# A one-core encoder trunk: down projection regrouped into parts of 6, 4, 8 and 4 tiles, and a new price list for the planner

## The chip, the cores and the metric

The kernel runs on one core of a Trainium2 chip. The metric is device time in microseconds (us). Three runs of the kernel before gave 1074.99, 1075.91 and 1076.12 us, median 1075.91. Engines are named as the profile names them: PE (matrix products) with PEld (its weight loads), DVE, ACT, POOL and SP; SP and POOL also issue the transfers (DMA).

## What is computed

A layer works on 512 prompt tokens and 64 sample tokens, 576 columns of 1024 features:

```
x += Mixer(RMSNorm(x))       # gated delta rule (4 heads) and gated linear attention (4 heads), gated merge
x += CrossAttn(RMSNorm(x))   # 4 heads into 256 memory tokens
x += ConvFFN(RMSNorm(x))     # what the change touches
y  = RMSNorm(x)

def conv_ffn(h):                               # D_FF = 2816 = 22 tiles of 128
    u = h @ w_up                               # (576, 2*2816): gate half and value half
    u = causal_dwconv(u, width=3) + conv_b
    return (silu(u_gate) * u_val) @ w_down     # (576, 2816) @ (2816, 1024)
```

Recurrent states, the last rows of both convolutions and the memory keys and values are outputs too.

## The kernel before

**Arithmetic.** Everything is held feature-major: a tile is 128 features by the 576 token columns. Weights and activations are float32, and each is split into a high and a low half (`w` tiles hold both; `xh`/`xl`, `ach`/`acl` and `hl` are activations), so that one product of 128 features costs three matmuls: high by high, low by high, high by low. A **plain** product handles the 576 columns as two matmuls of 256 and 320 columns (2 x 290 in the up projection, which pads to 580). **Seven products** handle a pair of output tiles at once: columns are halved (288, or 290), input tiles are taken in pairs, and the eight block products of a 2 x 2 by 2 x 2 block multiplication are replaced by seven (named P1, Q5, P2, Q6, P3, Q7, Q4). It needs sums of weight blocks (`ws` tiles, four sums for a pair, made on DVE), sums of activations (`tu`, `tw`, made in `operands`), and seven additions of results instead of four.

**Feed-forward stage.** `up j` makes gate tile j and value tile 22 + j from `yops` (products) or from `yx` (plain); the result goes through the norm's scale (`fu<-fu,rbc`), three taps of the convolution (`fc`), SiLU and the gate product, and is split again (`acl<-fc,ach`). `down (m, p)` multiplies part p of those 22 tiles into output tile m of x. `PARTS` (L96) cuts the 22 tiles into four parts, here of 6, 6, 4 and 6. `NPLAIN` (L128) is the count of plain up pairs, `DNPLAIN` (L129) names the parts whose down products are plain, and `DNAT` (L130) says after which up pair how many pairs of the part before are multiplied. Of the last part, tiles 2 to 5 go as seven products, tiles 0, 1 ("last") and 6, 7 (`half`, L2318) plain. `ffn_order` (L135) turns this into one fixed list.

**Weights.** A weight comes by a DMA into a `wr` tile; ACT writes the high half (CAST) and minus the weight (ACTIVATE) and POOL issues a DMA that adds the weight again (`split_summed`, L717), or ACT writes the high half of a sum and DVE (at times POOL) subtracts (`w<-ws,w`). There are ten `w` tiles and four `wr` tiles (L30 to L33), and 64 slots (`NS`, L29) for all other wide tiles.

**What sets the order.** A planner in the program (`Driver`) keeps a clock for every engine while the kernel is written down. PE's instructions stand in the order in which `main` yields them, with the steps of side chains (the delta rule `c_gdn`, the norms, the attention) slipped in when the planner has their inputs ready. An instruction of DVE, ACT or POOL is booked into the first gap of its engine after its inputs are ready (`place`, L374); with a rank from `URGENT` (L40) it may push lower ones back (`ahead`, L405). The engine then gets its instructions in the order of the planned starts. `weigh` (L219) prices an instruction; `HOP` (L35) is the delay assumed from one engine's end to another's start; `note` (L447) and `hold` (L482) book. The planner's prices thus set the order of instructions and nothing else: every wait on the chip is a semaphore on the real producer.

Of the kernel before, what the change touches and what calls it, by code (L numbers as in the profile page):

```python
# [31 lines left out]
WF = 4  # L32
RF = 1  # L33
NGDN = 2
HOP = 0.2  # L35
BACK = 6.0
MARGIN = 0.6
LAG = 0.0
# [54 lines left out]

PARTS = [list(range(0, 6)), list(range(6, 12)), list(range(12, 16)), list(range(16, 22))]  # L96
PARTK = [p[0::2] + p[1::2] for p in PARTS]
PART0 = [0, 6, 12, 16]
def product_order(pairs, whole=False):


# [23 lines left out]
XAT = ("qb", 1)  # L125
XLAG = 30.0
GPAIRS = [(("gta", m), ("gtb", m)) for m in range(GPLAIN, 8)]
NPLAIN = 3  # L128
DNPLAIN = (0, 1, 2)  # L129
DNAT = (0,) * 6, (0, 0, 0, 2, 1, 1), (0, 2, 1, 1), (0, 0, 0, 0, 1, 1)  # L130
UPAIRS = [(("up", j), ("up", NJ + j)) for j in range(NPLAIN, NJ)]
HALVED = {t for p in GPAIRS + WPAIRS + MPAIRS + UPAIRS for t in p}

# [76 lines left out]
class Engine:  # L210
# [8 lines left out]
    def weigh(self, calls):  # L219
        cost, aps, outs = 0.0, [], []  # L220
        for name, args, kw in calls:
            a = [v for v in list(args) + list(kw.values()) if hasattr(v, "tensor")]
            ins = [v for v in a[1:] if free(v) > 1]
            n = max(free(v) for v in a)
            if kw.get("op") == ALU.pow:
                cost += 0.3 + 0.165 * free(a[0])
            else:
                twice = self.key == "V" and len(ins) == 1 and self.port([(name, args, kw)])
                cost += self.drv.FIXED[self.key] + n * self.drv.PACE[self.key] * (0.5 if twice else 1.0)
            cost += 0.06 * (name == "scalar_tensor_tensor" or self.key == "V" and a[0].shape[-1] <= 128 and any(v.space == bass.MemoryType.PSUM for v in a[1:]))  # L230
            cost += 0.2 * (kw.get("accum_out") is not None) + 0.09 * hasattr(kw.get("scale"), "tensor")
            outs.append(a[0])
            if kw.get("accum_out") is not None:
                outs.append(kw["accum_out"])
            aps += a
        return cost, outs, aps
# [11 lines left out]

    def when(self, calls):
        cost, outs, aps = self.weigh(calls)  # L250
        return self.drv.place(self.key, self.drv.open(outs, aps), cost, False, self.port(calls)) + cost

    def together(self, calls, extra=0.0):

        cost, outs, aps = self.weigh(calls)
        self.drv.note(self.key, cost + extra, outs, aps, [(getattr(self.eng, name), args, kw) for name, args, kw in calls], self.port(calls))


class Either:
# [20 lines left out]
class Driver:  # L280

    FIXED = dict(V=0.15, A=0.17, G=0.2, D=0.01)
    PACE = dict(V=1 / 960, A=1 / 1180, G=1 / 465, D=512 / 320e3)

# [117 lines left out]
    def ahead(self, key, t, cost, port=False, op=None):  # L405

        q = self.busy[key]
        t = max(t, self.now - BACK)
        i = 0
        while i < len(q):  # L410
            o = q[i]
# [5 lines left out]
            if o.start < t or o.level >= op.level:  # L417
                t, i = o.end, i + 1
# [9 lines left out]
            if stuck is None:  # L428
                for o, at in moves:
                    self.shift(o, at)  # L430
                break
            t, i = q[i].end, i + 1
        self.book_op(q, op, t, cost, port)
        q.sort(key=lambda o: o.start)
        return t
# [11 lines left out]
    def note(self, key, cost, outs, aps, fns, port=False):  # L447
        op = Op()
        t = self.open(outs, aps)
        op.level = self.urgent  # L450
        start = (self.ahead if op.level else self.place)(key, t, cost, port=port, op=op)
        end = start + cost
        self.before(start, outs, aps)
        self.mark(self.wrote, end, outs, op)
        self.mark(self.seen, end, aps, op)
# [26 lines left out]
    def hold(self, fn, cost, args, kw):  # L482
# [4 lines left out]
        self.put(self.now, [(fn, args, kw)])  # L487
        self.now += cost
        self.mark(self.seen, self.now, ins)
        self.mark(self.wrote, self.now, [out])  # L490
        self.last = max(self.last, self.now)
        self.flush(self.now - BACK)

    def array(self, out, lhsT, rhs, exact=True):
# [6 lines left out]
        self.mode, self.half = mode, None if beside else at  # L501
        if beside:
            return 0.01
        return turn + (max(n * 0.0004375 + 0.008, 0.109) if fast else 0.107 if not exact else max(n * 4 / 2400, 0.107))

    def matmul(self, out, lhsT, rhs, **kw):
        self.hold(self.pe.matmul, self.array(out, lhsT, rhs), (out, lhsT, rhs), kw)
# [2085 lines left out]
```

## Time and profile before

| | |
|---|---|
| median of three runs | 1075.91 us |
| profiled execution, its own time | 1073.67 us |
| span of that execution, first to last instruction | 1071.9 us |
| mean granted clock of PE, as a share of 2.4 GHz | 0.997 |
| PE busy | 1059.0 us, 99% |
| DVE busy | 779.2 us, 73% |
| ACT busy | 722.9 us, 67% |
| POOL busy | 336.0 us, 31% |

Almost every operation is recorded by one helper line (L314), so groups are told apart by their tiles: `bank` and `sm` are PSUM tiles, `w` weights, `x` the residual stream, `fu` and `fc` the up projection before and inside its convolution. Matmul records overlap (each shows its whole pipeline), so the pace of PE is read from the distance of starts and not from the mean of one. The feed-forward stage runs from about 667 us to the end.

### The profile page before, as it was taken

To read this page: it belongs to the slowest core of one execution; us is meant where nothing else is said; L and a number is where in the kernel's file an instruction comes from. 1 tells how busy PE (TensorE), PEld (TensorE's weight loads), DVE (VectorE), ACT (ScalarE), POOL (GpSimd) and SP (SyncE) were. 2 spreads that over 40 slices of the span, in tenths; PEclk is the share of its full clock that TensorE was granted. 3 is DMA by queue.
4 is the path that set the end of the run, shared out by engine and by line. 5 is a ranking of instruction groups with operands and counts; after the bars stand their busy time and mean duration, and the time that the engine had idled before them with its cause. 6 is when DMAs were issued, how large, how long until landed. Compare 5 with 4: busy or idle time off the path is not lost.

```text
span 1071.9 us, 21256 instructions
## 1 busy us (share of the span) xinstructions
PE 1059.0 (99%) x8086; PEld 1041.1 (97%) x8086; DVE 779.2 (73%) x1518; ACT 722.9 (67%) x1435; POOL 336.0 (31%) x529
## 2 busy tenths in 40 slices
PE   9999999999999999999999999999999999999997
PEld 8999999999999999999999999999999999999996
DVE  5776657677786869877647777888885765788874
ACT  7767456765766766465755768877876666687753
POOL 2343045322433224121110134334434233333420
PEclk9999999999999999999999999999999999999999
DMA  8854137643366987688873558758898798878863
GB/s 279 188 119 102 29 99 179 174 101 82 63 150 140 205 231 199 209 190 221 220 196 91 127 141 199 173 120 183 172 214 191 156 191 185 176 159 169 195 125 104
DMA packets 67813, 172.77 MB, mean 161 GB/s; under 512 B 7872, under 2 KB 14912, under 8 KB 67712
## 3 DMA queue, kind: packets, MB, share of 16 engines
q0 software_dynamic: 30816, 71.32, 39.1%
q1 hardware_dynamic: 36752, 100.09, 28.7%
q8 instruction: 64, 1.05, 0.4%
q14 instruction: 37, 0.30, 0.1%
q10 hardware_dynamic: 144, 0.00, 0.0%
HBM read 158.81 MB, written 5.37 MB: 153 GB/s over the span
## 4 chain that ended last, share of the span: by engine, by line
PE 93%; DMA 2%; DVE 2%; issue 1%; ACT 1%; POOL 1%; SPq 0%; DVEq 0%; POOLq 0%; ACTq 0%
PE bank L314 62%; PE sm L314 31%; DMA wr<-wt 1%; DMA w<-wt 1%; DMA vec<-vec 1%; DVE ws L314 0%; ACT w L314 0%; ACT sq L314 0%; POOL rr L314 0%; DVE w L314 0%; SPq L314 0%; DVE c L314 0%; DVE gt L314 0%; DVE rr L314 0%; ACT xh L314 0%
## 5 line engine op out<-in xcount | busy, mean ns | idle before, releaser
L314 PE MATMUL bank<-xh,w 128*128 128x320 f32 (+3 forms) x1664 | 316.9, 300 | 2.5 <-DVE u L314 1.7
L314 PE MATMUL bank<-ach,w 128*128 128x256 f32 (+3 forms) x1362 | 268.9, 296 | 0.0
L314 PEld LDWEIGHTS bank<-xh,w 128*128 128x128 f32 x1664 | 254.9, 189 | 4.4 <-ACT e L314 1.9
L314 POOL DMA_DIRECT2D w<-wt x152 | 133.9, 890 | 372.2 <-ACT w L314 296.0
L314 PEld LDWEIGHTS bank<-ach,w 128*128 128x128 f32 x1362 | 216.1, 188 | 0.7 <-issue 0.3
L314 PE MATMUL bank<-xl,w 128*128 128x256 f32 (+2 forms) x832 | 188.4, 296 | 0.3 <-DVE xl L314 0.3
L314 ACT CAST w<-wr 128x512 fp32r<-128x512 f32 (+4 forms) x208 | 157.9, 762 | 26.1 <-PE bank L314 19.7
L314 PE MATMUL bank<-acl,w 128*128 128x288 f32 (+3 forms) x681 | 168.1, 295 | 0.0
L314 ACT ACTIVATE w<-wr 128x512 fp32r<-128x512 f32 (+3 forms) x186 | 141.7, 763 | 9.8 <-PE bank L314 7.5
L314 PEld LDWEIGHTS bank<-xl,w 128*128 128x128 f32 x832 | 142.4, 189 | 0.6 <-DVE xl L314 0.6
L314 PE MATMUL sm<-ach,w 128*128 128x290 f32 (+1 forms) x618 | 133.2, 296 | 0.6 <-DVE x L314 0.6
L314 PEld LDWEIGHTS bank<-acl,w 128*128 128x128 f32 x681 | 121.8, 188 | 0.0
L314 ACT CAST w<-ws 128x512 fp32r<-128x512 f32 (+1 forms) x144 | 87.0, 610 | 28.7 <-DVE ws L314 13.4
L314 PEld LDWEIGHTS sm<-ach,w 128*128 128x128 f32 x618 | 102.6, 189 | 1.2 <-ACT w L314 0.8
L314 DVE TENSOR_TENSOR w<-ws,w 128x512 fp32r<-128x512 f32 (+1 forms) x112 | 75.7, 682 | 12.8 <-ACT w L314 12.0
L314 PE MATMUL sm<-acl,w 128*128 128x290 f32 (+1 forms) x309 | 84.7, 296 | 0.0
L314 DVE SCALAR_TENSOR_TENSOR fc<-fu,vec,fc 128x578 f32<-128x578 f32 x88 | 70.9, 816 | 4.5 <-ACT fc L314 4.0
L314 PEld LDWEIGHTS sm<-acl,w 128*128 128x128 f32 x309 | 58.2, 188 | 0.0
L314 DVE TENSOR_TENSOR x<-x,bank 128x256 f32<-128x256 f32 (+2 forms) x73 | 30.0, 442 | 28.2 <-PE bank L314 28.0
L314 DVE TENSOR_TENSOR ws<-ws,wr 128x512 f32<-128x512 f32 (+1 forms) x72 | 48.8, 678 | 0.4
L314 POOL DMA_DIRECT2D w<-wd x34 | 29.6, 872 | 61.6 <-ACT w L314 60.7
L314 ACT ACTIVATE fc<-fu,vec 128x578 f32<-128x578 f32 x44 | 38.3, 873 | 15.0 <-POOL fu L314 14.9
(394 smaller groups left out, 2066.2 us busy)
## 6 DMA issues: line engine op xcount, KB each, us to landing
wr<-wt SPq DMA_DIRECT2D x134, 512.0 KB, 5.4
w<-wt POOLq DMA_DIRECT2D x102, 256.0 KB, 5.5
w<-wt POOLq DMA_DIRECT2D x50, 512.0 KB, 7.0
wr<-wd SPq DMA_DIRECT2D x24, 384.0 KB, 5.3
w<-wd POOLq DMA_DIRECT2D x20, 384.0 KB, 6.4
w<-ws POOLq DMA_DIRECT2D x26, 256.0 KB, 3.8
x<-xT SPq DMA_DIRECT2D x16, 288.0 KB, 6.4
y<-xT SPq DMA_DIRECT2D x8, 288.0 KB, 5.7
```

The costliest lines, as they stand in the source:

```text
L314: fn(*args, **kw)
```

## The change

It does two things. First, the 22 tiles are cut into parts of 6, 4, 8 and 4 instead of 6, 6, 4 and 6; the second part (4 tiles) is multiplied as seven products for all four pairs of output tiles; the last part stays half and half; and one up pair more goes as seven products (two plain pairs instead of three). `DNAT` is set anew. Second, the planner's prices change: `HOP` falls from 0.2 to 0.06 with 0.14 (`PELAT`) added behind a matmul; each DVE and ACT instruction occupies its engine for 0.085 and 0.095 less than its result takes (`TAIL`); a scan costs twice per column; a DVE instruction with two SBUF inputs that is booked by rank starts after a POOL instruction that is under way (`VEXT`), and a POOL instruction grows by the DVE instructions that it overlaps (`GEXT`); a one-column matmul in full float32 costs 0.218.

```diff
-HOP = 0.2
+HOP = 0.06
+PELAT = 0.14
+GEXT = 1.0
+VEXT = True
...
-PARTS = [list(range(0, 6)), list(range(6, 12)), list(range(12, 16)), list(range(16, 22))]
+PARTS = [list(range(0, 6)), list(range(6, 10)), list(range(10, 18)), list(range(18, 22))]
-PART0 = [0, 6, 12, 16]
+PART0 = [0, 6, 10, 18]
...
-NPLAIN = 3
-DNPLAIN = (0, 1, 2)
-DNAT = (0,) * 6, (0, 0, 0, 2, 1, 1), (0, 2, 1, 1), (0, 0, 0, 0, 1, 1)
+NPLAIN = 2
+DNPLAIN = (0, 2)
+DNAT = (0,) * 6, (0, 0, 2, 2), (0, 0, 2, 2, 0, 0, 0, 0), (0, 0, 1, 1)
...
+            cost += n * self.drv.PACE[self.key] * (name == "tensor_tensor_scan")
...
-        self.drv.note(self.key, cost + extra, outs, aps, ...)
+        self.drv.note(self.key, cost + extra - self.drv.TAIL[self.key] * len(calls), outs, aps, ...)
...
+    TAIL = dict(V=0.085, A=0.095, G=0.0)
...
+        if port and key == "V" and VEXT:
+            t = max([t] + [o.end for o in self.busy["G"] if o.port and o.start < t])
...
+        if port and key == "G" and GEXT:
+            for o in self.busy["V"]:
+                if o.port and o.end > t:
+                    if o.start >= t + cost:
+                        break
+                    cost += GEXT * (min(o.end, t + cost) - max(o.start, t))
...
-        end = start + cost
+        end = op.end + self.TAIL[key]
...
-        self.mark(self.wrote, self.now, [out])
+        self.mark(self.wrote, self.now + PELAT, [out])
...
-        return turn + (... else max(n * 4 / 2400, 0.107))
+        return turn + (... else max(n * 4 / 2400, 0.107 if n > 1 else 0.218))
```

Counted over the whole program, PE loses 72 matmuls of 256 columns, 72 of 320 and 12 of 290, and gains 126 of 288 columns. DVE's instructions grow from 1520 to 1583, ACT's from 1338 to 1376, POOL's from 534 to 538; SP's stay at 247.

Two places show how the order moves. The first is DVE near 65 to 70 us. There `gc` is the scan of the gates, `rr` a column of four factors of the first delta-rule head, made from what POOL writes, and `u<-bank` takes a finished projection out of the PSUM banks. Before:

```order
L314 SCALAR_TENSOR_TENSOR gc_683<-scm_432,gy_448 128x576
L314 SCALAR_TENSOR_TENSOR gy_459<-gy_459,gna_460 128x576
L314 SCALAR_TENSOR_TENSOR gc_684<-scm_432,gy_459 128x576
L314 TENSOR_TENSOR qg_737<-qg_737,c_378 128x512
L314 TENSOR_TENSOR rr_728<-rr_728 128x4
L314 TENSOR_TENSOR rr_728<-rr_728,sg 128x4 x2
L314 SCALAR_TENSOR_TENSOR rr_728<-l_712,rr_728 128x4
L314 TENSOR_TENSOR dgt_738<-keep,rr_728 128x512
L314 TENSOR_TENSOR u_784<-bank_669,rbc_367 128x256
L314 TENSOR_TENSOR u_784<-bank_670,rbc_367 128x256
```

The same work in the changed program:

```order
L319 SCALAR_TENSOR_TENSOR gc_634<-scm_404,gy_419 128x576
L319 SCALAR_TENSOR_TENSOR gy_433<-gy_433,gna_434 128x576
L319 SCALAR_TENSOR_TENSOR gc_635<-scm_404,gy_433 128x576
L319 TENSOR_TENSOR u_719<-bank_600,rbc_367 128x256
L319 TENSOR_TENSOR qg_660<-qg_660,c_375 128x512
L319 TENSOR_TENSOR u_719<-bank_601,rbc_367 128x256
L319 TENSOR_TENSOR u_719<-bank_601,rbc_367 128x64
L319 TENSOR_TENSOR rr_651<-rr_651 128x4
L319 SCALAR_TENSOR_TENSOR rr_651<-l_626,rr_651 128x4
L319 TENSOR_TENSOR rr_651<-rr_651,sg 128x4 x2
```

The evacuation of the bank stood behind the five `rr` and `dgt` instructions and now stands ahead of them.

The second place is PE where the second part of the down projection begins, between two up projections (290 columns, from the `xh`/`xl` tiles and the `ach`/`acl` tiles of the norm's output). Before, after up pair 13, its first plain product with six input tiles:

```order
L314 MATMUL bank_10935<-xh_8371,w_10833 128x290
L314 MATMUL bank_10935<-xh_8481,w_10833 128x290
L314 MATMUL bank_11033<-ach_10031,w_10870 128x256
L314 MATMUL bank_11034<-ach_10031,w_10870 128x320
L314 MATMUL bank_11033<-acl_10032,w_10870 128x256
L314 MATMUL bank_11034<-acl_10032,w_10870 128x320
L314 MATMUL bank_11033<-ach_10187,w_10870 128x256
L314 MATMUL bank_11034<-ach_10187,w_10870 128x320
```

Now, after up pair 12, the first of its seven products, then a product of the up pair, then the second:

```order
L319 MATMUL bank_10819<-xh_8483,w_10711 128x290
L319 MATMUL sm_10929<-hl_9857,w_10733 128x288 x2
L319 MATMUL sm_10929<-hl_10158,w_10733 128x288 x2
L319 MATMUL sm_10929<-hl_9857,w_10733 128x288
L319 MATMUL sm_10929<-hl_10158,w_10733 128x288
L319 MATMUL bank_10776<-ach_8566,w_10754 128x290
L319 MATMUL sm_10960<-ach_10005,w_10775 128x288
L319 MATMUL sm_10960<-acl_10006,w_10775 128x288
```

A product of this part is six matmuls of 288 columns with a weight of its own; before, one weight served 36 matmuls of 256 and 320. From the end of the first part's down products to the start of the third part's, PE now has 924 matmuls of 290 columns (up pairs 10 to 20) and 168 of 288 (four pairs by seven products), and no plain product.

## Rows read from the trace of the kernel before

**Rows 1.** The page, busy time of PE: us, share of the span, instructions.

```profile
PE 1059.0 (99%) x8086; PEld 1041.1 (97%) x8086; DVE 779.2 (73%) x1518; ACT 722.9 (67%) x1435; POOL 336.0 (31%) x529
```

**Rows 2.** Waits of PE, whole span: total us, times, longest.

```profile
PE bank L314 <- DVE u L314: 1.7, 1, 1.7
PE warm L314 <- POOL mhalf L314: 1.0, 1, 1.0
...
PE sm L314 <- DVE x L314: 0.6, 1, 0.6
```

**Rows 3.** Stretches: length; busy PE, PEld, DVE, ACT, POOL; granted clock; DMA.

```profile
70.50:75.00 4.50, 4.39 (x23) 4.22 (x23) 1.69 (x8) 1.71 (x2) 2.50 (x6) 0.62 0.50 77
700.00:780.00 80.00, 80.00 (x597) 80.00 (x596) 70.62 (x121) 65.42 (x124) 33.32 (x53) 1.00 0.75 162
780.00:803.00 23.00, 23.00 (x176) 23.00 (x175) 20.61 (x36) 16.73 (x28) 7.61 (x12) 1.00 0.95 208
945.00:1008.00 63.00, 63.00 (x472) 63.00 (x471) 54.96 (x96) 49.71 (x91) 25.09 (x43) 1.00 0.82 182
```

**Rows 4.** Timeline of PE, a plain down product: start, us, instruction, count.

```profile
787.03 0.42 PE L314 MATMUL bank<-acl,w 128*128 128x256 f32 x2
...
789.66 0.42 PE L314 MATMUL bank<-acl,w 128*128 128x256 f32 x2
```

**Rows 5.** Timeline of PE, products of 288 columns.

```profile
1035.25 0.29 PE L314 MATMUL sm<-acl,w 128*128 128x288 f32 x1
...
1037.63 0.30 PE L314 MATMUL sm<-acl,w 128*128 128x288 f32 x1
```

**Rows 6.** Timeline of PE, up projection of 290 columns.

```profile
699.77 0.43 PE L314 MATMUL bank<-xh,w 128*128 128x290 f32 x2
...
702.47 0.71 PE L314 MATMUL bank<-xh,w 128*128 128x290 f32 x4
```

**Rows 7.** Timeline of POOL, DVE and PE around 65 to 71 us.

```profile
64.94 2.73 POOL L314 TENSOR_TENSOR rr<-l,mhalf 128x8 f32<-128x8 f32 x1
67.64 1.14 POOL L314 TENSOR_TENSOR e<-gc 128x576 f32<-128x576 f32 x1
...
67.70 1.11 DVE L314 TENSOR_TENSOR rr<-rr 128x4 f32<-128x4 f32 x1 [0.93 <-POOL rr L314]
68.84 0.37 DVE L314 TENSOR_TENSOR rr<-rr,sg 128x4 f32<-128x4 f32 x2
...
69.80 1.68 DVE L314 TENSOR_TENSOR u<-bank,rbc 128x256 f32<-128x256 f32 x6
...
70.36 0.85 PE L314 MATMUL bank<-xh,w 128*128 128x256 f32 x2 [1.71 <-DVE u L314]
```

**Rows 8.** DVE by form, 700 to 1043 us: count, busy us, mean ns.

```profile
L314 DVE SCALAR_TENSOR_TENSOR fc<-fu,vec,fc 128x578 f32<-128x578 f32 x85 | 68.5, 816 | 4.5 <-ACT fc L314 4.0
L314 DVE TENSOR_TENSOR w<-ws,w 128x512 fp32r<-128x512 f32 x53 | 36.2, 687 | 8.5 <-ACT w L314 8.4
L314 DVE TENSOR_TENSOR fu<-fu,rbc 128x580 f32<-128x580 f32 x38 | 28.8, 759 | 8.7 <-ACT fu L314 8.3
L314 DVE TENSOR_TENSOR fu<-fu,sm 128x290 f32<-128x290 f32 x33 | 15.0, 454 | 16.2 <-PE sm L314 16.1
L314 DVE TENSOR_TENSOR fc<-fc,fc 128x64 f32<-128x64 f32 x18 | 3.9, 219 | 0.0
L314 DVE TENSOR_TENSOR w<-ws,w 128x384 fp32r<-128x384 f32 x5 | 2.8, 555 | 0.2 <-ACT w L314 0.2
```

**Rows 9.** Timeline of DVE, instructions that follow each other without a gap.

```profile
965.42 0.82 DVE L314 SCALAR_TENSOR_TENSOR fc<-fu,vec,fc 128x578 f32<-128x578 f32 x1
966.16 0.69 DVE L314 TENSOR_TENSOR w<-ws,w 128x512 fp32r<-128x512 f32 x1
```

**Rows 10.** Timeline of DVE and PE at the last two products of the last pair.

```profile
1046.04 0.45 DVE L314 TENSOR_TENSOR x<-x,sm 128x288 f32<-128x288 f32 x1
...
1046.64 0.37 PE L314 MATMUL sm<-ach,w 128*128 128x288 f32 x1 [0.64 <-DVE x L314]
```

More of the change, by code (lines that the diff above doesn't have):

```diff
@@ L250, in when @@
         cost, outs, aps = self.weigh(calls)
-        return self.drv.place(self.key, self.drv.open(outs, aps), cost, False, self.port(calls)) + cost
+        return self.drv.place(self.key, self.drv.open(outs, aps), cost - self.drv.TAIL[self.key], False, self.port(calls)) + cost
     def together(self, calls, extra=0.0):
         cost, outs, aps = self.weigh(calls)
-        self.drv.note(self.key, cost + extra, outs, aps, [(getattr(self.eng, name), args, kw) for name, args, kw in calls], self.port(calls))
+        self.drv.note(self.key, cost + extra - self.drv.TAIL[self.key] * len(calls), outs, aps, [(getattr(self.eng, name), args, kw) for name, args, kw in calls], self.port(calls))
 class Either:
@@ L489, in hold @@
         self.mark(self.seen, self.now, ins)
-        self.mark(self.wrote, self.now, [out])
-        self.last = max(self.last, self.now)
+        self.mark(self.wrote, self.now + PELAT, [out])
+        self.last = max(self.last, self.now + PELAT)
         self.flush(self.now - BACK)
@@ L503, in array @@
             return 0.01
-        return turn + (max(n * 0.0004375 + 0.008, 0.109) if fast else 0.107 if not exact else max(n * 4 / 2400, 0.107))
+        return turn + (max(n * 0.0004375 + 0.008, 0.109) if fast else 0.107 if not exact else max(n * 4 / 2400, 0.107 if n > 1 else 0.218))
     def matmul(self, out, lhsT, rhs, **kw):
```

## The prediction

> **What bounds the kernel now.** I read the page first: PE is busy in 99% of the span [rows 1], DVE, ACT and POOL in 73, 67 and 31%. Next came the waits of PE: seven in all, from 1.7 to 0.3 us, and none of them between 667 and 1043 us, where the feed-forward stage runs [rows 2]. Then the stretches: while up projections run as seven products, PE is busy in 80.00 of 80 us and in 63.00 of 63 with DVE at 88 and 87% [rows 3]. So the length of the kernel is the sum of PE's matmuls at their pace plus a few waits, and DVE is the engine next to the limit. Two questions follow: how much PE work goes, and whether the other engines still keep up, in the new order and with the new parts.
>
> **PE's work.** Pace from distances of starts. In a plain product ten pairs of a 256 and a 320 column matmul start between 787.03 and 789.66 us: 0.263 us for a pair [rows 4]. Of 288 columns, 18 start between 1035.25 and 1037.63: 0.132 each [rows 5]. Of 290, 20 start between 699.77 and 702.47: 0.135 each [rows 6]. The counted change is 72 pairs away, 126 of 288 columns more, 12 of 290 less: -72 x 0.263 + 126 x 0.132 - 12 x 0.135 = -18.9 + 16.6 - 1.6 = **-3.9 us**. It splits into the second part as products, the last part shrinking from six to four tiles (it loses a third of its saving) and one up pair. All of it lies on the path as long as PE is what is waited for. The last plain products stand in the tail, where ACT and DVE write the output between them; if these fill the time that PE gives back there, up to 12 matmuls of about 0.13 us, 1.6 us, would not be gained. I keep the full sum, since PE and not they ends the tail's waits but for one.
>
> **The stall at 68 us.** The largest wait of PE is 1.7 us at 70.36, for a `u` that frees a PSUM bank [rows 7]. The cause stands in the rows before it. POOL's power on `rr` takes 2.73 us while DVE scans; DVE then waits 0.93 us for it, and its next instruction, four columns wide, takes 1.11 us instead of the 0.18 of its neighbours (0.37 for two), because POOL's 576-column operation has begun at 67.64. Only then, at 69.80, does DVE evacuate the bank. Behind the wait the clock falls: from 70.5 to 75 us the granted clock is 0.62 [rows 3], which between the levels of 2.4 and 1.2 GHz means 0.38/0.5 = 76% of 4.5 us at half pace, 1.7 us of work lost. The stall thus costs 1.7 + 1.7 = 3.4 us. In the changed order the evacuation stands ahead of `rr`, so what DVE waits for there no longer holds the bank. What is late next is `rr` itself, which the delta rule needs a few microseconds on, where PE has projections to do meanwhile. I take **-2.5 us**, between -3.4 (all of it) and 0 (another wait of the same size).
>
> The Trainium skill, in SBUF — State Buffer, "Who interferes with whom", says that a DVE instruction with two SBUF inputs and a POOL instruction that reads SBUF share a read port as an exclusive lock, held by whichever starts first for its whole length. The trace agrees: DVE's four columns end at 67.70 + 1.11 = 68.81 us, just behind POOL's 67.64 + 1.14 = 68.78. By that rule the new booking (DVE behind a POOL instruction under way) describes the chip and the old one by rank did not; this bears on the chance of the large gain below.
>
> **The rest of the new order.** Every stretch between 20 and 670 us is interleaved anew, with 0.06 or 0.2 us between engines where 0.2 was assumed, and shorter occupancy. The trace supports the shorter occupancy: two DVE instructions start 0.74 us apart where the first takes 0.82 [rows 9]. A tighter plan brings matmuls of the side chains forward, and each may arrive before its operand. Before, seven waits make some 5 us; as many new ones may come or as many go. I take 0, with 3 us either way.
>
> **The short products.** Where two products of a pair follow each other with nothing between, PE waits until DVE has read the bank: 0.64 us at the very end [rows 10]. In the new part a product is six matmuls, 6 x 0.132 = 0.8 us, before 1.2 (last part) or 1.6 (up). Between a product and the next that writes its bank stand two or three others, 1.6 us or more, against some 0.8 us for PE's end, the 0.45 of the addition and the restart; one instruction of 0.75 in front of the addition uses it up, two make PE wait. Six pairs now have such products. Bounds: 0, and 6 x 0.64 = 3.8. I take **+0.8**, nearer to 0 because up products beside them stretch most of the distances.
>
> **DVE between the parts.** A pair of up tiles gives DVE four sums and three subtractions of 512 columns, three additions of 290, two scalings and one split (0.75), four taps (0.82) and the gate product in two pieces: 7 x 0.687 + 3 x 0.454 + 3 x 0.759 + 4 x 0.816 + 0.687 + 0.219 = 12.6 us in 19 instructions [rows 8]. With 0.08 less for each that follows another [rows 9] it is 11.1, against PE's 84 x 0.135 = 11.3. A pair of down tiles with four input tiles gives seven operations of 256 columns (0.687 - 2 x (0.687 - 0.555) = 0.42 each) and seven additions of 288 (0.455, as for 290): 6.1 us, at pitch 5.0, against PE's 42 x 0.132 = 5.5. The operands of the part cost some 6 us more, at pitch 5. So between the first and the third part's plain products DVE has 11 x 12.6 + 4 x 6.1 + 6 = 169 us by durations and 11 x 11.1 + 4 x 5.0 + 5 = 147 by pitch; PE has 924 x 0.135 + 168 x 0.132 = 147. Work can be put off: in the plain stretch from 780 to 803 DVE is still 20.6 of 23 us busy [rows 3], though the four plain output tiles there (two additions each, under 0.5 us apiece) and the weights of the next up pair ask for some ten us of it, so that about 11 us of postponed taps were carried into it while PE never stopped. The price lies between 0 (pitch) and 169 - 147 - 11 = 11 us (durations). I take the end nearest to rows 9, **0**, since DVE's queue there is dense. ACT, at 82% from 700 to 780, gets 13 us more over some 340: nothing. POOL issues two more transfers and SP none: nothing.
>
> **The sum.** -3.9 - 2.5 + 0 + 0.8 + 0 = -5.6 us. The profiled execution took 1073.67 us, 1.8 more than its span; with the sum 1068.1. That execution lies 2.2 below the median of the runs, so against 1075.91 the forecast is **1070.3 us**.
>
> **The rivals.**
> - *PE's saving alone.* New waits in the front half take back what the one at 68 us gave. For it: every order there is new and the plan is tighter. Against: the rows name one cause, and its instructions are moved. -3.9 + 0.8 = -3.1: 1072.8.
> - *All waits go.* The plan now books the port as the chip does. The waits behind the start are some 4 us with the half clock's 1.7 on top: -3.9 - 6 + 0.8 = -9.1: 1066.8. Against: the waits at the tail and for weights have other causes.
> - *DVE takes it back.* Half of its bound, 5.5 us, appears as waits of PE among up pairs 13 to 20: -0.1: 1075.8, no change. For it: 147 against 147 leaves no room for the gaps that make 12% of DVE's time in [rows 3]. Against: those gaps did not hold PE up, and ten weight tiles and the postponed taps lie between.
> - *DVE bounds the stretch, slower.* Without plain products between up pairs 10 and 20 DVE works at its durations, the postponed work fills the slots, and weights come late: -5.6 + 11 = +5.4: 1081.3. It decides once the waits pass 5.6 + 2.2 = 7.8 us. For it: 169 us of work. Against: rows 9 are the pitch in just such a stretch.
>
> The Trainium skill's page TensorE: Matmul & The Clock Gate, Part 1, holds that the clock is low by default and that activity raises it, so that a pause costs twice. The 0.62 behind the stall agrees. It makes any new wait of the front half dearer than it looks and is why I leave 3 us either way.
>
> **How the numbers follow.** Chances: the forecast 0.53, PE's saving alone 0.20, all waits go 0.08, DVE takes it back 0.11, DVE bounds 0.08. The forecast's own range is 1068 to 1072.7. For 8 in 10 I take 1065.8 to 1076.0: it holds the forecast, the second and most of the third, and reaches to the fourth. About 0.2%, 2.2 us, is what a measurement of this kernel tells from no change, so faster means under 1073.7: nearly all of the first (0.52), most of the second (0.16) and the third: 0.76. The rest of these and the fourth make no change: 0.15. Slower is the last and a little of the fourth: 0.09.
>
> **What would show it.** In the profile after, PE's busy time falls by about 4 us and the wait of `bank` for `u` at 70 us is gone, with the clock at 1.00 from 57 to 80 us: the first two terms. DVE's busy share between the parts rises to 95% or more with PE's at 100%: the term of 0. The additions `x<-x,sm` of 288 columns end few and short waits of PE. The forecast is wrong if PE waits for `w` or for DVE by more than a microsecond between 760 and 930 us, or if the front half lists as many waits as before. A down product that starts late because its `acl` is not ready would point to the fourth and fifth case.

## The result, and the profile after

Six runs of the changed kernel took 1079.08 to 1084.89 us, median **1080.01**; the kernel before beside it took 1075.57. The ratio is 1.0052 (95% interval 1.0036 to 1.0068): about 4.4 to 5.6 us slower, where 1070.3 had been forecast. The profiled execution is the slowest of the six (1084.89), so its rows show more loss than the median has.

From the page (answers to [rows 1]): PE's busy time did not fall by four microseconds, it rose by two, and its share fell.

```profile
PE 1061.1 (98%) x8056; PEld 1038.0 (96%) x8056; DVE 800.2 (74%) x1581; ACT 730.4 (67%) x1473; POOL 329.8 (30%) x533
```

The waits of PE in the whole span (answers to [rows 2]; total us, times, longest): eighteen kinds where there were seven waits. `bank` for `u` is gone; `fu` and `gx` are new, and the waits for the transfer of a weight (`w`, listed under the second stretch) grow from one of 0.7 us to four of 4.4 us.

```profile
PE sm L319 <- ACT fu L319: 3.5, 5, 1.6
...
PE sm L319 <- ACT gx L319: 1.5, 1, 1.5
...
PE bank L319 <- ACT fu L319: 1.1, 1, 1.1
```

Stretches of the kernel after (columns as in [rows 3]):

```profile
20.00:660.00 640.00, 637.33 (x4956) 621.37 (x4955) 460.04 (x955) 416.26 (x884) 172.58 (x285) 1.00 0.63 152
60.00:80.00 20.00, 20.00 (x160) 20.00 (x159) 15.46 (x38) 12.20 (x20) 9.45 (x20) 1.00 0.64 139
70.50:75.00 4.50, 4.50 (x38) 4.50 (x37) 3.10 (x8) 2.89 (x7) 1.19 (x4) 1.00 0.46 91
680.00:800.00 120.00, 115.03 (x841) 112.78 (x840) 104.61 (x182) 93.30 (x169) 50.35 (x73) 1.00 0.76 164
860.00:900.00 40.00, 39.34 (x293) 38.87 (x291) 38.62 (x82) 32.05 (x73) 19.13 (x29) 1.00 0.84 170
860.00:1010.00 150.00, 145.30 (x1062) 143.53 (x1060) 128.92 (x235) 112.42 (x218) 55.98 (x90) 0.99 0.80 176
880.00:920.00 40.00, 38.21 (x275) 37.97 (x274) 34.16 (x67) 29.25 (x61) 15.25 (x22) 0.96 0.87 193
```

and of the kernel before, the same three long ones:

```profile
20.00:660.00 640.00, 636.44 (x4948) 621.85 (x4941) 458.41 (x948) 415.49 (x890) 186.90 (x291) 1.00 0.62 152
680.00:800.00 120.00, 120.00 (x898) 120.00 (x897) 105.21 (x181) 96.17 (x172) 46.62 (x77) 1.00 0.79 173
860.00:1010.00 150.00, 150.00 (x1125) 150.00 (x1124) 112.61 (x194) 107.20 (x192) 55.05 (x87) 1.00 0.83 179
```

PE's idle time is the length less its busy time. From 20 to 660 us it is 2.67 us against 3.56, and the half clock at 70 us is gone (1.00 where 0.62 stood). In the feed-forward stage PE stood still in neither long stretch before; now it idles 120 - 115.03 = 4.97 us in the first (680 to 800 us) and 4.70 in the second (860 to 1010). These two numbers are used below as the measure of each run. They undercount: a wait of 1.57 us (below) puts 1.87 us between two starts that stand 0.135 apart otherwise, 1.73 lost, and behind the longest one the clock is 0.96 of 40 us, at half pace for 8% of it, 1.6 us more. This execution also has a half clock near its start:

```profile
24.00:28.00 4.00, 4.00 (x21) 3.97 (x22) 1.81 (x7) 0.63 (x3) 3.24 (x11) 0.57 0.98 236
```

0.43/0.5 of 4 us at half pace are 1.7 us of work. Three kernels below that keep the instruction order of this one (e5, e6, e11) show 1.00 there, so this belongs to the execution and not to the order.

**First stretch.** Its two longest waits, at 735.77 and 749.63, end the same chain of instructions, which runs twice. The timeline of POOL, then of ACT, then of PE (start, us, instruction, the wait before it):

```profile
729.00 2.70 POOL L319 COPY fout<-fu 128x4 f32<-128x4 f32 x1
...
742.34 2.70 POOL L319 COPY fout<-fu 128x4 f32<-128x4 f32 x1
744.98 0.80 POOL L319 COPY fu<-fst 128x4 f32<-128x4 f32 x1
```

```profile
745.81 0.88 ACT L319 ACTIVATE fc<-fu,vec 128x578 f32<-128x578 f32 x1 [1.63 <-POOL fu L319]
746.58 0.62 ACT L319 ACTIVATE w<-ws 128x512 fp32r<-128x512 f32 x1
747.10 0.60 ACT L319 CAST w<-ws 128x512 fp32r<-128x512 f32 x1
747.61 0.63 ACT L319 ACTIVATE w<-wr 128x512 fp32r<-128x512 f32 x1
748.14 0.60 ACT L319 CAST w<-wr 128x512 fp32r<-128x512 f32 x1
748.65 0.61 ACT L319 CAST w<-ws 128x512 fp32r<-128x512 f32 x1
749.17 0.40 ACT L319 ACTIVATE fu<-sm 128x290 f32<-128x290 f32 x1
```

```profile
735.77 0.40 PE L319 MATMUL bank<-xh,w 128*128 128x290 f32 x1 [1.08 <-ACT fu L319]
...
749.63 0.40 PE L319 MATMUL sm<-xh,w 128*128 128x290 f32 x1 [1.57 <-ACT fu L319]
```

Read backwards: PE needs a PSUM tile (`sm`) that ACT empties at 749.17; that stands behind five instructions on weights and one `fc`, which waited 1.63 us for a four-column copy of POOL; and that copy came late because the copy before it took 2.70 us (the median of the 44 of its kind is 0.18). A stretched copy of POOL thus reaches PE through ACT's queue.

**Second stretch.** Here PE waits for split weights. The waits of PE from 860 to 1010 us; the kernel before has none there:

```profile
PE bank L319 <- DMA w<-wt: 1.8, 1, 1.8
PE bank L319 <- DMA w<-wd: 1.5, 2, 1.1
PE sm L319 <- DMA w<-ws: 1.1, 1, 1.1
PE sm L319 <- ACT fu L319: 0.3, 1, 0.3
```

The short products of the second part (288 columns) stand between 859 and 906 us. Only the longest of the waits for weights, at 901 us, lies among them; the others, at 958, 982 and 1007, come 50 to 100 us behind, one in an up product, two in plain products of the third part.

What ACT waits for before it can write a weight tells where the way of a weight is late. In the kernel before, and in the changed one, 860 to 1010 us:

```profile
ACT w L314 <- DVE ws L314: 6.8, 6, 3.4
...
ACT w L314 <- PE bank L314: 6.1, 7, 2.3
```

```profile
ACT w L319 <- DVE ws L319: 9.6, 11, 1.9
```

For PE to give back a split tile, ACT waited 6.8 us before (6.1 and 0.7 for `sm`) and waits 1.1 now (0.7 and 0.4). For DVE's sums it waits longer than before. So, as far as these waits tell, free tiles are there; it is what goes into them that is late.

And at the end one wait for `gx`, 1.55 us where `x` cost 0.64 [rows 10]:

```profile
1062.92 0.38 PE L319 MATMUL sm<-ach,w 128*128 128x288 f32 x1 [1.55 <-ACT gx L319]
```

### The profile page after: what moved, and what is told of

Read it like the earlier page. It is cut to its first block, busy times and chain, and to the rows that moved or that the text cites. A ratio compares the mean times of both kernels' runs of the same rounds, so it can differ in the third digit from the quotient of the medians.

```text
span 1082.8 us, 21369 instructions
## 1 busy us (share of the span) xinstructions
PE 1061.1 (98%) x8056; PEld 1038.0 (96%) x8056; DVE 800.2 (74%) x1581; ACT 730.4 (67%) x1473; POOL 329.8 (30%) x533
## 5 line engine op out<-in xcount | busy, mean ns | idle before, releaser
L319 PE MATMUL bank<-xh,w 128*128 128x256 f32 (+3 forms) x1584 | 305.0, 302 | 4.1 <-DMA w<-wt 1.8
L319 PEld LDWEIGHTS bank<-xh,w 128*128 128x128 f32 x1584 | 243.0, 189 | 7.0 <-DMA w<-wt 2.0
L319 PE MATMUL bank<-xl,w 128*128 128x256 f32 (+3 forms) x792 | 179.5, 297 | 0.5 <-DVE xl L319 0.5
L319 ACT CAST w<-wr 128x512 fp32r<-128x512 f32 (+3 forms) x213 | 157.3, 741 | 15.4 <-DMA wr<-wt 8.2
L319 PE MATMUL sm<-ach,w 128*128 128x288 f32 (+1 forms) x616 | 135.1, 299 | 3.5 <-ACT gx L319 1.5
L319 PEld LDWEIGHTS bank<-xl,w 128*128 128x128 f32 x792 | 136.0, 189 | 1.4 <-DVE xl L319 1.4
L319 ACT CAST w<-ws 128x512 fp32r<-128x512 f32 (+1 forms) x164 | 94.5, 584 | 36.9 <-DVE ws L319 16.0
L319 DVE TENSOR_TENSOR w<-ws,w 128x512 fp32r<-128x512 f32 (+1 forms) x129 | 83.6, 653 | 30.4 <-ACT w L319 29.0
L319 PE MATMUL sm<-acl,w 128*128 128x288 f32 (+1 forms) x308 | 85.6, 298 | 0.0
L319 PE MATMUL sm<-xh,w 128*128 128x290 f32 x208 | 46.5, 298 | 2.7 <-ACT fu L319 2.7
```

The lines of the kernel that those rows point to most:

```text
L319: fn(*args, **kw)
```

## The experiments

Theory 1: the new prices took away slack. Theory 2: the new parts make the stage too dense. Later A, B and C name causes within the stage: DVE's rate, the weights' way, the order. Idle is PE's, first stretch / second stretch, in us (before 0 / 0, after 4.97 / 4.70).

**Parts or prices?** Each half alone.

```
e1: before.py + the new PARTS, PART0, NPLAIN, DNPLAIN, DNAT
e2: after.py  + the old PARTS, PART0, NPLAIN, DNPLAIN, DNAT
```

> The kernel before with the new parts alone (6, 4, 8, 4 tiles, second part and half of the last as seven products, two plain up pairs) and the old prices. The change gives 4.4 us more, although PE's work falls by 3.9 and the stall at 68 us (3.7 with the clock behind it) is gone: so some 12 us of new waits have come. Theory 1 (the new prices took away the slack that hid late weights and late evacuations): the waits stay away, 1075.6 - 3.9 + 0.8 = about 1072.5 us, few waits of PE between 667 and 1043 us. Theory 2 (the new parts make DVE and ACT too dense in the feed-forward stage): the waits come here, 1075.6 - 3.9 + 12 = about 1083.7 us, or, since half of the waits lie in the front, at least 1077.

Measured 1099.73 us, ratio 1.0222 (1.0202 to 1.0242); idle 4.80 / 14.33.

> The changed kernel with the old parts (6, 6, 4, 6, three plain up pairs) and the new prices. Theory 1 (prices): no saving of PE's work, the stall at 68 us gone, 12 us of new waits: 1075.6 - 3.7 + 12 = about 1083.9 us, at the least above 1079, with PE waiting for fu and for w in the feed-forward stage. Theory 2 (parts): the feed-forward stage runs without waits as before and only the front half differs: 1075.6 - 3.7 = about 1072 us.

Measured 1078.88, ratio 1.0030 (1.0016 to 1.0044); idle 1.55 / 0.00. So the parts bring the loss, 24 us with the old prices; the prices alone cost 3.3, and with the new parts they give 20 back. Theory 1 falls as the main cause, and the two halves don't add; theory 2's own numbers (1083.7 and 1072) were missed as well. The waits of PE in the parts-only kernel, 660 to 1040 us, name both down products that lack `ach` and weights that come late:

```profile
PE bank L314 <- ACT ach L314: 5.4, 3, 2.4
PE bank L314 <- DMA w<-ws: 5.1, 3, 2.5
PE sm L314 <- DMA w<-wt: 2.9, 1, 2.9
PE sm L314 <- DMA w<-ws: 2.3, 2, 1.5
```

**Which price?** In the changed kernel, one price at a time back to the old.

```diff
 e3: -TAIL = dict(V=0.085, A=0.095, G=0.0)   +TAIL = dict(V=0.0, A=0.0, G=0.0)
 e4: -HOP = 0.06, PELAT = 0.14               +HOP = 0.2, PELAT = 0.0
```

> The changed kernel with TAIL at 0 for DVE and ACT: each of their instructions is booked for its whole duration again; everything else as changed. Theory 1, if it is the shortened occupancy that overfills the plan of ACT and DVE: the waits for fu, gx and xl go, about 1080 - 8 = 1072 us. Theory 1, if it is the delay between engines: no change, 1079 to 1081. Theory 2 (parts): no change or a little, above 1078.

Measured 1102.18, ratio 1.0244 (1.0222 to 1.0266); idle 4.99 / 13.76.

> The changed kernel with the old delay between engines: HOP 0.2 and PELAT 0; everything else as changed. What a DVE or ACT instruction assumes of a matmul stays the same sum (0.06 + 0.14 = 0.2 + 0); what a matmul assumes of them, and they of each other, goes back to 0.2. Theory 1, if it is this margin that hid late operands: about 1072 us and few waits of PE. Theory 1, if it is the occupancy: 1079 to 1081. Theory 2 (parts): no change or a little, above 1078.

Measured 1085.00, ratio 1.0090 (1.0072 to 1.0109); idle 4.28 / 10.64. Neither new price made the waits: without the shorter occupancy the changed kernel is 22 us slower, without the shorter delay 5. The expectations of theory 1 missed in all four runs.

With the old parts, the rules for the port (with the scan and the one-column matmul), and these plus the delays:

```diff
 e8:  after.py, old parts, TAIL 0, HOP 0.2, PELAT 0
 e12: after.py, old parts, TAIL 0, HOP 0.06, PELAT 0.14
```

> The kernel before (old parts, HOP 0.2, no TAIL, no PELAT) with the planner's rules for the port that DVE and POOL share alone (VEXT, GEXT), the doubled scan and the price of a one-column matmul. If these moved the evacuation of u ahead of rr, the stall at 68 us goes (3.4 to 3.7 us) and nothing else is tighter: about 1072 us. If the shorter occupancy (TAIL) or the shorter delay moved it: the stall stays, 1075 to 1076 us.

Measured 1073.76, ratio 0.9988 (0.9975 to 1.0001); idle 0.75 / 0.00. The stall at 70 us is gone; of its 3.4 us one is seen.

> The kernel before (old parts) with the new delays between engines (HOP 0.06, PELAT 0.14) and the port's rules, but whole occupancy (no TAIL). The prices with all parts old gave 1078.9, the port's rules alone 1073.8: the 5 us between them are the delay or the occupancy. If the delay: about 1078 us. If the occupancy: about 1073.5 us.

Measured 1077.27, ratio 1.0016 (0.9999 to 1.0032); idle 0.00 / 0.00, but 1.6 us between 660 and 680. The kernel before had medians of 1074.35 to 1075.98 beside the groups of runs, so kernels of different groups are compared by their ratios: with the old parts the short delay costs some 3 us (1.0016 against 0.9988; the difference of the times, 3.5, holds some of that shift), the occupancy 1.5 more (1.0030).

**DVE or the weights' transfers?** Two kernels with every instruction of every engine in the changed kernel's order, and one suspect made smaller. e5 leaves the convolution unfinished and e6 three quarters of the low halves, so their times are those of less work; they serve to place the loss.

```diff
 e5, up_conv, last tap only:
-V.scalar_tensor_tensor(c[:, 0:CW], u[:, i:i + CW], ...)
+V.scalar_tensor_tensor(c[:, 0:64], u[:, i:i + 64], ...)   # booked as 578 columns
 e6, accumulate, from 640 us on:
-dma_start(out, in_, accum_op=add)
+dma_start(out[:, 0:n // 4], in_[:, 0:n // 4], accum_op=add)
```

> The changed kernel with every engine's instructions in the same order, but the last tap of each of the 44 convolutions in the feed-forward stage covers 64 columns instead of 578 (so the convolution is left unfinished): 44 x about 0.65 = 29 us less of DVE's work there, nothing else. Theory A (DVE's rate is the bound of the stretch of products without plain work, and all the lateness of weights and evacuations comes from it): of the 14.3 us that PE loses in that stage at most 4 stay, 1080 - 10 = about 1070 us. Theory B (a weight's way from ACT over POOL's queue to its last transfer is too long for the ten weight tiles, 0.8 us each in a short product): the loss stays, 1078 to 1080 us. Theory C (the order itself: an instruction stands behind another that waits): part of it stays, about 1075.

Measured 1075.17, ratio 0.9999 (0.9980 to 1.0017); idle 0.41 / 4.06.

> The changed kernel with every engine's instructions in the same order, but each transfer that adds a weight for the low half moves a quarter of its columns in the feed-forward stage (so three quarters of these low halves are wrong): the transfers become shorter, POOL's issues stay. Theory A (DVE's rate): little goes, since the transfers were late only because DVE was; 1077 to 1080 us. Theory B (the weights' transfers are the bound): the waits for w go and with them most of the 14.3 us, about 1070 us. Theory C (order): only the four waits that end on a transfer (1.8, 1.5, 1.1 and some) shrink, about 1076.

Measured 1075.39, ratio 1.0003 (0.9988 to 1.0017); idle 3.52 / 0.32. They gave 4.8 and 4.6 us, where theories A and B each had one give 10 and the other next to nothing. Theory C, the order, had forecast both times (1075 and 1076); they alone do not tell it from two causes. The stretches tell more: the rows of the two kernels, first the short tap, then the short transfer.

```profile
680.00:800.00 120.00, 119.59 (x891) 119.24 (x890) 95.91 (x182) 95.50 (x172) 45.26 (x76) 1.00 0.82 182
860.00:1010.00 150.00, 145.94 (x1078) 144.13 (x1077) 113.89 (x222) 110.15 (x207) 52.84 (x86) 1.00 0.81 180
```

```profile
680.00:800.00 120.00, 116.48 (x852) 114.26 (x852) 103.67 (x181) 94.43 (x171) 49.68 (x74) 1.00 0.47 106
860.00:1010.00 150.00, 149.68 (x1119) 149.28 (x1118) 128.12 (x235) 113.32 (x216) 56.12 (x89) 1.00 0.50 119
```

A relieved DVE clears the first stretch and leaves the second; a shorter transfer clears the second, where DVE is as busy as before (128.12 us), and leaves most of the first (3.52 of 4.97). Two stretches, two causes. Both at once:

> The changed kernel with the same order and both relieved: last tap of 64 columns in the feed-forward stage (the convolution unfinished) and a quarter of the columns in the transfers that add the weights there (these low halves wrong). If DVE in the first stretch and the weights' transfers in the second are the whole loss, the two gains of 4.8 and 4.6 us add: 1080 - 9.4 = about 1070.5 us, with under 2 us lost in the stage. If both had shortened the same waits: 1073 to 1075.

Measured **1070.05**, ratio 0.9940 (0.9920 to 0.9960); idle 0.38 / 0.32. The gains add, and of the idle time in the two stretches 0.7 us is left, so nothing of that size is left there for an order that is bad by itself. The time is near the forecast of 1070.3, but of a kernel that does less; the kernel before with the same two things made smaller was not run.

**The second part plain, and the third plain up pair.**

```diff
 e7:  -DNPLAIN = (0, 2)   +DNPLAIN = (0, 1, 2)
 e9:  -NPLAIN = 2         +NPLAIN = 3
 e10: both
```

> The changed kernel with the second part plain again (parts of 6, 4, 8, 4 and the new prices stay): PE gets 8 x 24 plain matmuls for 4 x 42 of products, 25.2 - 22.2 = 3.0 us more work; DVE loses some 25 us (seven additions and seven operations on weights a pair, and the operands). Theory A (DVE's rate): the loss of 14.3 us falls by two thirds, 1080 + 3 - 9 = about 1074 us, and PE no longer waits between 860 and 960 us. Theory B (short products eat the weight tiles faster than they come): the same there, but the waits near 735 and 750 us and those behind 975 stay: about 1076. Theory C (order): 1080 + 3 = 1083, less what the new order does.

Measured 1083.43, ratio 1.0078 (1.0054 to 1.0103); idle 4.35 / 1.85. The second stretch loses 2.9 less, and what it still loses is one new wait, for `fu` (PE's waits from 860 to 1010 us):

```profile
PE sm L319 <- ACT fu L319: 1.9, 1, 1.9
```

No wait for a weight is left, not at 958 and 982 us either: with the short products of the second part the late weights go. PE works 3.0 us more, and by the medians the kernel is 3.4 us slower: nothing won. The time is theory C's (1083), not A's or B's, and shows that the idle time of single profiles does not add up to medians.

> The changed kernel with three plain up pairs as before (parts and prices stay as changed): PE gets 12 x 0.135 = 1.6 us more work. By now the loss of PE in the feed-forward stage falls into two stretches: 680 to 800 us, 7 us, which a shorter tap nearly takes away (DVE) and a shorter weight transfer does not; and 860 to 1010 us, 7 us, which a shorter weight transfer takes away and a shorter tap does not. Theory A for the first stretch (the third plain pair was what let DVE prepare operands ahead): the loss before 800 us falls from 7 to 1 to 2.5 us, the second stretch keeps its 7: 1080 + 1.6 - 5 = about 1076.5 us. Rival (the prices alone make that loss): the first stretch keeps 7 us: about 1081.6.

Measured 1080.23, ratio 1.0043 (1.0028 to 1.0058); idle 0.83 / 7.15. The first stretch did as theory A said, and so it does in every run: with the new parts, the kernels with three plain pairs lose 0.74 to 0.90 us there (e9, e10, e14, e15, e17), those with two 2.85 to 4.99, but for the two with the short tap. The second stretch lost 2.5 more, so that the time stayed. That is not the rule: in the two pairs further down (e13 and e14, e16 and e17) the third plain pair makes the kernel 2.9 and 5.3 us faster.

> The changed kernel with three plain up pairs and the second part plain: of the change only the cut into 6, 4, 8, 4 tiles and the prices are left; 1.6 + 3.0 = 4.6 us more of PE's work than as changed. If the two stretches add, both losses go but for the 3.8 us near 980 us that the kernel with the second part plain had: 1080 + 4.6 - 14.3 + 2 + 3.8 = about 1076 us. If the new cut itself costs, above 1079.

Measured 1080.84, ratio 1.0044 (1.0028 to 1.0059); idle 0.90 / 2.88, all of the second stretch in two waits for `fu`. In idle time the stretches add; the time is not the 1076 that was expected then, but that of the other branch, that the new cut itself costs. Against the old cut under the same prices (e2, 1.0030) the intervals overlap, and 0.7 us of the difference is PE's work, so a cost of the cut is not shown either.

**What is short in the second stretch?** First the low halves of the short products' weights by DVE instead of by a transfer (e14 with three plain pairs, e15 also with the old delays):

```diff
-if prod in ("P1", "P2", "Q4") or prod == "Q5" and pair[0][0] != "gta":
+if pair[0][0] != "dn" and (prod in ("P1", "P2", "Q4") or prod == "Q5" and pair[0][0] != "gta"):
```

> The changed kernel with the low halves of the short products' weights (down projection, 256 columns) made by a subtraction on DVE for all seven products instead of by a transfer for four of them: up to 24 transfers of 128 KB fewer, 24 subtractions of 0.42 us more on DVE (some 10 us), the sums exact as before. Theory B (the weights' transfers bound the second stretch, 860 to 1010 us, and their number is what matters): of the 7 us lost there at most 3 stay, PE no longer waits for w of ws or wd of 128 KB: 1080 - 4 = about 1076 us. Rival 1 (the bytes matter, not the number: 128 KB transfers are a tenth of all bytes there): no change, 1079 to 1081. Rival 2 (DVE has no room there after all): slower, above 1081.

Measured 1082.11, ratio 1.0067 (1.0048 to 1.0087); idle 2.85 / 6.17.

> The same with three plain up pairs. In the kernel with three plain pairs alone the first stretch lost 1.8 us and the second 11. Theory B (number of transfers): the first keeps its 1.8, the second falls to 3 to 4: 1080.2 - 7 = about 1073 us. Rival 1 (bytes): 1079 to 1081, the second stretch keeps most of its 11. Rival 2 (DVE has no room): above 1081.

Measured 1079.18, ratio 1.0048 (1.0032 to 1.0064); idle 0.78 / 5.05.

> The kernel with three plain pairs and the low halves of the short products on DVE, and the old delays between engines (HOP 0.2, PELAT 0). With the old parts the new delays cost 1077.3 - 1073.8 = 3.5 us; with the new parts the old ones cost 5. If the delay's cost is a matter of the front half and of the tail alone: about 1073 - 2 = 1071 us. If the new parts need the short delays whatever the weights do, because lateness of DVE decides the order: about 1078 us.

Measured 1076.70, ratio 1.0019 (1.0007 to 1.0030); idle 0.74 / 5.47. The times fit rival 2 (e13), rival 1 (e14) and neither branch (e15). The second stretch keeps its loss with up to 24 small transfers fewer, but not the same waits: PE's waits for weights there fall from 4.4 to 2.2 us (e13 against the changed kernel) and from 6.8 to 1.4 (e14 against e9), and waits for `fu` and `x` come, 4.0 and 3.6 us. (In e15 the weights have 3.6.) So fewer transfers did relieve the weights in e13 and e14, and DVE, now busy in 39.24 of the 40 us from 860 to 900 (e13), probably took back what they gave. The old delays, which cost 5 us in e4, gain 2.5 here (e15 against e14): what a delay costs hangs on the rest of the plan.

In the kernel with short transfers it is the time of each that changed: they land sooner, and so do the raw loads beside them, which were not touched. Transfers from 860 to 1010 us (queue, count, size, median us from issue to landing), in the kernel before, as changed and with the short transfers:

```profile
wr<-wt SPq DMA_DIRECT2D x14, 512.0 KB, 5.6
w<-wt POOLq DMA_DIRECT2D x25, 256.0 KB, 6.5
```

```profile
wr<-wt SPq DMA_DIRECT2D x17, 512.0 KB, 6.1
w<-wt POOLq DMA_DIRECT2D x27, 256.0 KB, 5.2
...
w<-wd POOLq DMA_DIRECT2D x9, 128.0 KB, 6.1
```

```profile
wr<-wt SPq DMA_DIRECT2D x16, 512.0 KB, 4.2
...
w<-wt POOLq DMA_DIRECT2D x27, 64.0 KB, 3.8
```

Before, the same transfers took as long, with the DMA engines at 0.83 (0.80 as changed), and PE waited for none of them. So slower transfers are not what is new; there was time for them, and now there is not.

Then the tiles: one split weight tile given for one raw tile.

```diff
-WF = 4    -RF = 1
+WF = 3    +RF = 2      # e16; e17 with NPLAIN = 3; e18 with the old parts and the port's rules
```

> The changed kernel with one raw weight tile more and one split weight tile less (five wr, nine w) in the same room. A pair of short products holds two of four raw tiles for some 5.5 us, half of what an up pair holds them, while the load takes 6 us and the way to the split weight as long again. Theory B1 (the raw tiles are too few, so that loads start late): the second stretch (860 to 1010 us) loses 2 us instead of 7: about 1075 us. Theory B2 (the transfers themselves share the DMA engines and each takes too long, whenever it starts): no gain, 1079 to 1081. Theory B3 (the split tiles are what is short): slower, above 1081.

Measured 1097.57, ratio 1.0190 (1.0162 to 1.0218); idle 3.01 / 10.39, and 8.39 instead of 2.67 between 20 and 660.

> The same with three plain up pairs, where the first stretch lost 1.8 us and the second 11. Theory B1: the second stretch falls below 4 us, 1080.2 - 7 = about 1073 us. Theory B2: 1079 to 1081. Theory B3: above 1081.

Measured 1092.23, ratio 1.0151 (1.0121 to 1.0181); idle 0.84 / 12.42.

> The control: the old parts with the port's rules (1073.8 us) and five raw, nine split tiles. The feed-forward stage lost 1.4 us there. Theory B1 and B2: no change, 1073 to 1075. Theory B3 (split tiles short): some us more, above 1076.

Measured 1074.20, ratio 0.9982 (0.9968 to 0.9996); idle 0.29 / 0.00. With one split tile of ten less the second stretch loses 5 to 6 us more (10.39 for 4.70, 12.42 for 7.15). B1's times (1075 and 1073) missed and B3's came true in the first two runs; what the raw tile gives by itself is not shown, since a split tile went with it. B3's forecast for the control (above 1076) missed: there nothing is lost. But the control has the old prices too, and of the 17.6 us in e16 nearly six lie ahead of 660 us, where the new prices and not the parts set the order, and 4.2 more between 1010 and 1045; old parts with the new prices and nine tiles were not run, so the 5 to 6 are not shown to be the parts' alone. The waits from 860 to 1010 us in the kernel with nine split tiles, PE's for weights, and ACT's, which now waits for PE to give back a tile before it can write the next weight:

```profile
PE sm L319 <- DMA w<-ws: 6.1, 5, 2.2
PE bank L319 <- DMA w<-ws: 2.4, 2, 1.6
```

```profile
ACT w L319 <- PE sm L319: 7.7, 2, 7.3
ACT w L319 <- PE bank L319: 2.1, 1, 2.1
```

For a tile ACT waits 9.8 us here, 7.3 of it at once, and 1.1 in the changed kernel; in the control it waits 11.1, but never more than 1.9 at once, and PE loses nothing. So with these parts a tile less costs time; that ten were too few is not shown, and no run has eleven. The last control is also the only complete kernel here that is faster than before by an interval that leaves out no change, if by little: the old parts, the port's rules and five raw tiles, 0.18% (0.04 to 0.32). That the raw tile does it is not shown: with four (e8) it was 0.12%, and the intervals overlap.

## Why the prediction was wrong

Point by point, by its own terms.

- *PE's work, -3.9:* held as far as it can be seen. Span of both relieved (e11) less span before: 1068.0 - 1071.9 = -3.9. In it lie -1.7 of the half clock, -0.25 of idle time between 20 and 660 us (3.31 for 3.56), +0.7 of the two stretches and +0.9 of the last wait; -3.5 is left for the work.
- *The stall at 68 us, -2.5:* right in its mechanism: the wait and the half clock behind it are gone, and the front half gives 3.56 - 2.67 = 0.9 of idle time and 1.7 of clock, 2.6. As a gain in time it is less sure: the port's rules alone (e8) remove the stall and gain 1.2 us, by an interval from 2.7 to nothing.
- *The rest of the new order, 0 with 3 either way:* too narrow, and in the wrong place. With the old parts the prices cost 3.3 us where -2.5 was due, nearly 6 from the rest, and what can be placed of it in e2 lies mostly behind 660 us: 1.6 us of idle time in the first stretch and 1.1 from 1010 to 1045. The tighter delay is some 3 of it (e12 against e8).
- *The short products, +0.8:* the size came out for another reason. The last wait grew by 0.9, for `gx` and not for `x` (with both relieved it is as long and put down to `x`); elsewhere the additions `x<-x,sm` do not stop PE in the changed kernel.
- *DVE between the parts, 0; ACT, POOL, SP "nothing":* **this is the step that failed.** The parts cost 24 us with the old prices and leave PE idle for 9.7 us in the profile with the new. Half of that is DVE, but ahead of the new products: in the first stretch, where the prediction had booked nothing but the saving of one up pair. That pair was 1.6 us of PE's time and also DVE's lead; three plain pairs bring the idle time from 4.97 to 0.83. The other half was costed at nothing with the words that POOL issues two more transfers and SP none. What the runs show in its place is split weights that land too late for PE: 4.4 of the 4.70 us end on a transfer of a weight, and they go when these transfers move a quarter (0.32) and when the second part is plain again. Not the number of transfers grew but the pace at which weights are used up. A tile lasts 12 x 0.135 = 1.6 us in an up product and 6 x 0.132 = 0.8 in a short one; from 859 to 906 us, 28 short and 13 up products make that 1.1 us a tile by estimate, and the transfer into a tile alone takes 5.2 us at the median, 6.1 for the small ones. The prediction used those 0.8 us for the banks only. Which link ahead of the transfer is late (ACT waits 9.6 us for DVE's sums, and still 9.5 with the short tap), and why weights are late again 50 us behind the last short product, stays open.
- *The rivals:* the last of them (the fifth case), given 0.08, was nearest in size (1081.3) and in its last words, that weights come late; its cause, DVE's durations, is not borne out for the second stretch: the short tap leaves 4.06 of 4.70 us there. Of the signs named beforehand, PE's wait at 70 us is gone as said, but PE's busy time, which was to fall by 4 us, rose by 2. Two of the signs of a wrong forecast came: the front half lists seven waits for four (2.4 us in all, for 3.4), and PE waits for `w` by more than a microsecond between 760 and 930 us (1.8 at 901 us). DVE reaches 97% in 860 to 900 us (38.62 of 40), but PE isn't at 100% there.

The sum in the profiled execution: -3.9 - 2.6 + 0.9 + 9.7, with 1.6 of half clock behind the wait that ends at 901 us, some 3 for what idle time undercounts (an estimate) and the 1.7 of half clock at 24 to 28 us, is +10.4 against 1084.89 - 1073.67 = +11.2. The other 0.8 I can't place. The median lies 4.9 us below this execution; how much of each term it has isn't shown.

**Left open:** why whole occupancy costs 22 us with the new parts (e1, e3) and nothing with the old (e8). A plan that believes DVE to need 169 us where it needs 147 puts instructions in another order; which of these moves costs what was not tried. Nor is it shown how much of the first stretch is DVE's rate and how much POOL's stretched copies, since the short tap relieves both: the copies of 2.70 us are gone there, and also with the short transfers, where 3.52 us of idle time stay, so they are not the greater part. Theory C, the order, is not excluded as the way in which lateness is passed on: the chain through ACT's queue in the first stretch is of that kind.

## What to carry to other kernels

Before a product is made shorter, set the new time per weight tile against all that prepares one: here 0.8 us instead of 1.6, while the last transfer alone takes 5 to 6. Where the user of a tile waits, look at the engine that writes the tiles: if it seldom waits for a free one, as here with ten, what fills them is late, and not their number is the first suspect. A step that costs the bounding engine time can be what gives the next one its lead, so price it with both. And a loss of many small waits is best split by making one suspect smaller with the order held fixed; the stretches then show which waits belong to whom.

## What the hardware showed that was not expected

- A four-column copy of POOL took 2.70 us instead of 0.18, twice. It starts 0.02 us ahead of four DVE instructions without a gap, and ends with them. In the kernel before the longest of these copies took 1.99 us, at 701 us. The four:

```profile
729.02 0.69 DVE L319 TENSOR_TENSOR w<-ws,w 128x512 fp32r<-128x512 f32 x1
729.62 0.76 DVE L319 TENSOR_TENSOR fu<-fu,rbc 128x580 f32<-128x580 f32 x1
730.30 0.69 DVE L319 TENSOR_TENSOR ws<-wr 128x512 f32<-128x512 f32 x1
730.90 0.75 DVE L319 TENSOR_TENSOR acl<-fc,ach 128x576 fp32r<-128x576 f32 x1
```

- All four take both inputs from SBUF. By the Trainium skill (SBUF — State Buffer, "Who interferes with whom") a DVE instruction with two SBUF inputs contends with a GpSimd instruction that reads SBUF, and issue order decides who blocks. The trace agrees that they collide; by the starts of the records POOL came first, by 0.02 us, and was held up all the same, so who was first is not told at that distance. The rows add that POOL did not get its turn between four DVE instructions that follow each other.
- From 860 to 1010 us, transfers of 128 KB (`wd`) landed no sooner than those of 256 KB (`wt`; 6.1 and 5.2 us; over the whole kernel 4.4 and 5.6), and raw loads of an unchanged 512 KB came down from 6.1 to 4.2 us when other transfers moved a quarter.
